# Inverse's step products moved out of a three-buffer scratch ring, and the FFN's gate product on POOL in rounds 16 to 20

## The chip, the cores and the metric

The kernel runs on one core of a Trainium2 chip. The metric is device time in microseconds of one execution. The time before is 573.6 us, the median of three runs (573.47 to 574.25).

## The reference, cut to what matters

One decoder block on x of 256 tokens and 1,024 features, in float32. Everything that the change touches is in these lines:

```python
h = x @ W_in                                   # split into q,k,v,z,... of two attentions
v = silu(causal_dwconv(h_v))                   # 8 heads of 128 features
# gated DeltaNet, chunks of 64 tokens, 8 heads x 4 chunks = 32 systems
a_mat = I + strictly_lower(k_beta k^T * decay)  # 64 x 64 each
sol   = triangular_solve(a_mat, rhs)
...
# ConvGLU, 2 x 2816 columns
u = causal_dwconv(x @ ffn_w_up) + b;  u_gate, u_val = split(u)
f = (silu(u_gate) * u_val) @ ffn_w_down
x = layer_norm(alpha * x + f)
```

## The kernel before

**Products.** Every weight chunk is 128x1024 float32, streamed from HBM by the SP queue into a ring of six `raw` buffers. ACT writes its rounded part `hi` (line 192), DVE the rest `lo` (line 197); `hi` and `lo` have three buffers each. A feature product `mm_feat` (lines 319 to 321) is 24 matmuls of 256 columns into one of two PSUM buffers `pg`; the buffer is free again when ACT and DVE have read it.

**Convolution.** After each q, k or v product, `conv` has ACT write the scaled product into a scratch tile `cv` (line 146) and DVE add three shifted terms to it (line 351, three instructions, each reading `pg` in PSUM and `cv` in SBUF). A `Silu` on ACT follows one product later. In the FFN the same helper makes `ug` and `uv` with two shifted terms each.

**Scratch ring.** `scr()` hands out tiles of 128x512 from one ring of three buffers (`tag="scr", bufs=3`), whatever their name: `cv`, `ug`, `uv`, `hp`, `A`, `y`, `itmp` and others. A request takes the buffer of the third request before it, and waits for that one's last use.

**Order of the work.** All engines run in program order; the Python code writes that order out. The feature products are the backbone. The attention pieces are generators that `pump()` advances by a step after each product, and the table `WAITS` says how many pumps a step is held back. So what PE, ACT and DVE do for the attention stands in their queues at a fixed place among the products.

**The inverse.** `delta()` inverts the triangular systems. The diagonal 16x16 blocks are inverted first, on POOL, by 15 elimination steps (lines 580 to 585): step j multiplies a column of the block with a row of the inverse so far into `itmp` (line 581) and subtracts that from the rows below in `VN` (line 583), at most 8x8 = 64 columns. The result goes out to HBM and back in two other layouts (lines 589 and 592, two DMAs each from the POOL queue); ACT and DVE spread these into `T` and `TT`, both parts of the tile `LT` (ACT at line 146, DVE at line 602), and PE starts the next level of blocks from them at line 615. While POOL works, PE computes the products v0, v1, ... `itmp` is requested from the ring just before the requests of `hp`, of v0's `cv` and of v1's `cv`.

**The attention's memory.** `AT` is a tile of 128x4608 float32: the input at first, then weight chunks, later the attention's exponentials, `e6` (columns 4096 to 4455) and `er` (4456 to 4515). Columns 4096 to 4607 also hold squares of q and k for the norms (line 452), which PE reads before the inverse begins (line 458).

**The FFN.** Round j = 0 to 21 makes the products ug and uv of 128 features each. ACT takes `Silu` of ug; DVE multiplies it with uv into f (line 1319); ACT rounds f into `fh` (line 1323); DVE writes the rest `fl` (line 1324). Rounds 1 to 15 also carry the down product of the round before; the seven last down products (15 to 21) run after round 21, from chunks that are split in rounds 20, 21 and behind them into `YD`, `latemisc`, `latev` and the ring. In rounds 2 to 9 POOL does two 128x256 operations a round (`affine1`, lines 1260 and 1261); in rounds 10 to 21 it has no work.

Of the kernel before, what the change touches and what calls it, by code (L numbers as in the profile page):

```python
# [10 lines left out]
OP = mybir.AluOpType  # L11
# [7 lines left out]
NFF = FF // 128  # L19
# [30 lines left out]
TAIL = 7  # L50
# [49 lines left out]
class Body:  # L100
# [363 lines left out]
    def delta(self):  # L464
        nc = self.nc
# [105 lines left out]
        nc.gpsimd.dma_start(sl.rearrange("u p j -> p u j"), Lc)  # L571
        yield from self.wait("lw")
        nc.gpsimd.dma_start(vf[:, 256:512], sl.rearrange("u (b i) j -> (u b) (i j)", b=8))
        tmp = self.scr("itmp")
        nc.vector.memset(Xi[:, 0], 0.0)
        nc.vector.memset(vf[:, 512:768:17], 1.0)
        yield from self.wait("inv")
# [448 lines left out]
    def run(self):  # L1026
        nc, A = self.nc, self.A
# [203 lines left out]
        def first_up(w, t):  # L1231
            wt = up0[w].rearrange("p (k m) -> p k m", k=8)
            ts = slice(128 * t, 128 * t + 128)
            for k in range(8):
                nc.tensor.matmul(pg0[w][:, ts], wt[:, k], x1T[:, k, ts], start=(k == 0), stop=(k == 7))
# [22 lines left out]
        def affine1(n):  # L1258
            t, sl = n // 4, slice(256 * (n % 4), 256 * (n % 4) + 256)
            nc.gpsimd.tensor_tensor(x1[:, t, sl], res[:, t, sl], lnp[:, 0, sl], op=OP.mult)  # L1260
            nc.gpsimd.tensor_tensor(x1[:, t, sl], x1[:, t, sl], lnp[:, 1, sl], op=OP.add)
# [25 lines left out]
        def down(j, ns=range(5)):  # L1287
            if j == 0:
                for n in range(4):
                    pd[n] = self.ps("pdn")  # L1290
                pd[4] = self.psum.tile([128, 512], F32, name="pdn", tag="o", bufs=1)
            if j not in dch:
                dch[j] = self.next_chunk("dn", j)
            for n in ns:
                down_mm(j, n)
            if ns[-1] == 4:
                self.done_chunk("dn", j)
                self.ahead(most=1 if j > NFF - TAIL + 1 else 3)

        for j in range(NFF):  # L1300
            uu = []
            for w, n in enumerate(("ug", "uv")):
                if j:
                    hi, lo = self.next_chunk(n, j)
                    pg = self.mm_feat(hi, lo, X)
                    self.done_chunk(n, j)
                else:
                    first_up(w, 1)
                    self.done_chunk(n, 0)
                    pg = pg0[w]  # L1310
                c = w * NFF + j
                u = self.scr(n)[:, :256]
                self.conv(pg, u, fcw[:, c], fcb[:, c:c + 1])
                uu.append(u)
                if j + w < NFF:
                    self.ahead(most=1 if j > NFF - TAIL + 1 else 3)
            self.act(uu[0], uu[0], AF.Silu)
            f = uu[0]
            nc.vector.tensor_tensor(f, uu[0], uu[1], op=OP.mult)
            if j == NFF - 1:  # L1320
                self.ahead(most=1)
            fh, fl = Y[:, 0, j % 8], Y[:, 1, j % 8]
            nc.scalar.copy(fh, f)
            nc.vector.tensor_tensor(fl, f, fh.bitcast(F32), op=OP.subtract)
            fs[j] = (fh, fl)
            self.ahead(most=1 if NFF - 1 > j > NFF - TAIL + 1 else 3)
            if 0 < j <= NFF - TAIL:
                down(j - 1)
            if 1 < j < 10:
                affine1(j - 2)  # L1330
# [192 lines left out]
```

## Time and profile before

| | us |
|---|---|
| median of three runs | 573.6 |
| the profiled execution | 573.08 |
| its span, first to last instruction | 571.3 |
| PE busy | 554.5 |
| DVE busy | 394.1 |
| ACT busy | 306.7 |
| POOL busy | 110.3 |

The profiled execution took 1.8 us more than its span, the part before the first and after the last instruction. Busy time is the sum of an engine's instructions, overlaps counted once. Times in the rows are counted from the start of the span. In a timeline, a row's start and length are followed by the engine, the line of the code, the tiles (written <- read), the count and, in brackets, the idle time of the engine before it with what ended it.

### The profile page before, as it was taken

How to read it: one execution, taken by the hardware profiler on the slowest of the kernel's cores; microseconds unless marked ns; L12 is line 12 of the kernel's file. 1: busy time of each engine (PE TensorE's matmuls, PEld its weight loads, DVE VectorE, ACT ScalarE, POOL GpSimd, SP SyncE). 2: the span in 40 equal slices, each digit the busy share in tenths (PEclk: the TensorE clock that was granted, in tenths of full speed). 3: DMA queues.
4: the chain of work that ended last, by engine and by line, in shares of the span. 5: the costliest groups of instructions: out<-in, count | busy, mean ns of one | idle time of the engine just before them, and what ended most of it. 6: DMA issues, size and time to landing. Idle time of an engine off the chain costs nothing.

```text
span 571.3 us, 11612 instructions
## 1 busy us (share of the span) xinstructions
PE 554.5 (97%) x4585; PEld 508.8 (89%) x4585; DVE 394.1 (69%) x683; ACT 306.7 (54%) x575; POOL 110.3 (19%) x160
## 2 busy tenths in 40 slices
PE   8999999999799999999999999999999999999994
PEld 6999999988798898888898898899999999999974
DVE  2888745766686563467657487788777777778884
ACT  4656544624464446564677344465655555556651
POOL 2466632017401130004001000068000000000003
PEclk9999999999899999999999999999999999999998
DMA  8985548765552233223354645735655555555601
GB/s 317 406 305 180 190 146 278 287 211 185 145 182 93 76 112 111 76 73 112 112 185 128 242 148 183 258 102 180 209 185 191 191 180 192 186 189 172 200 3 73
DMA packets 28182, 99.94 MB, mean 175 GB/s; under 512 B 3340, under 2 KB 3996, under 8 KB 27740
## 3 DMA queue, kind: packets, MB, share of 16 engines
q1 hardware_dynamic: 27312, 95.94, 49.1%
q0 software_dynamic: 672, 2.93, 1.7%
q8 instruction: 36, 0.59, 0.4%
q10 hardware_dynamic: 144, 0.33, 0.1%
q14 instruction: 18, 0.15, 0.1%
HBM read 97.33 MB, written 1.46 MB: 173 GB/s over the span
## 4 chain that ended last, share of the span: by engine, by line
PE 77%; DVE 9%; ACT 6%; POOL 3%; issue 2%; DMA 2%; POOLq 0%; SPq 0%; DVEq 0%; ACTq 0%
PE pg L319 18%; PE pg L321 17%; PE pg L320 17%; PE pdn L1284 3%; PE pdn L1285 3%; PE pdn L1283 3%; DVE lo L197 2%; ACT hi L192 2%; PE poa L959 2%; PE pwo L1002 1%; PE pwo L1001 1%; PE pwo L1000 1%; ACT AT L146 1%; POOL itmp L581 1%; POOL VN L583 1%
## 5 line engine op out<-in xcount | busy, mean ns | idle before, releaser
L197 DVE TENSOR_TENSOR lo<-raw,hi 128x1024 fp32r<-128x1024 f32 (+1 forms) x147 | 179.2, 1221 | 75.3 <-ACT hi L192 74.4
L192 ACT CAST hi<-raw 128x1024 fp32r<-128x1024 f32 (+1 forms) x151 | 154.6, 1028 | 36.5 <-PE pg L320 9.8
L319 PE MATMUL pg<-X,hi 128*128 128x256 f32 x496 | 144.3, 291 | 4.8 <-ACT cv L146 4.8
L321 PE MATMUL pg<-X,lo 128*128 128x256 f32 x496 | 140.3, 283 | 0.0
L320 PE MATMUL pg<-X,hi 128*128 128x256 f32 x496 | 140.2, 283 | 0.0
L319 PE MATMUL pg<-Y,hi 128*128 128x256 f32 x400 | 113.0, 283 | 0.0
L320 PE MATMUL pg<-Y,hi 128*128 128x256 f32 x400 | 112.7, 282 | 0.0
L321 PE MATMUL pg<-Y,lo 128*128 128x256 f32 x400 | 112.5, 281 | 0.0
L319 PEld LDWEIGHTS pg<-X,hi 128*128 128x128 f32 x496 | 94.1, 190 | 9.7 <-ACT cv L146 4.9
L320 PEld LDWEIGHTS pg<-X,hi 128*128 128x128 f32 x496 | 94.2, 190 | 0.3 <-issue 0.2
L321 PEld LDWEIGHTS pg<-X,lo 128*128 128x128 f32 x496 | 94.1, 190 | 0.1
L320 PEld LDWEIGHTS pg<-Y,hi 128*128 128x128 f32 x400 | 75.3, 188 | 0.3 <-issue 0.2
L319 PEld LDWEIGHTS pg<-Y,hi 128*128 128x128 f32 x400 | 75.3, 188 | 0.2 <-issue 0.2
L321 PEld LDWEIGHTS pg<-Y,lo 128*128 128x128 f32 x400 | 75.3, 188 | 0.0
L351 DVE SCALAR_TENSOR_TENSOR cv<-pg,ppk,cv 128x255 f32<-128x255 f32 (+2 forms) x72 | 34.6, 481 | 17.4 <-ACT cv L146 15.7
L1359 POOL TENSOR_TENSOR NQ<-NQ,AT 128x512 f32<-128x512 f32 x2 | 2.6, 1298 | 159.7 <-ACT NQ L146 159.7
L1284 PE MATMUL pdn<-lo,X 128*128 128x512 f32 (+1 forms) x90 | 31.6, 351 | 0.0
L1283 PE MATMUL pdn<-hi,X 128*128 128x512 f32 (+1 forms) x90 | 31.5, 350 | 0.0
L1285 PE MATMUL pdn<-hi,X 128*128 128x512 f32 (+1 forms) x90 | 31.4, 349 | 0.0
L910 POOL TENSOR_SCALAR AT<-AT,sums 128x128 f32<-128x128 f32 (+1 forms) x12 | 10.9, 918 | 95.3 <-DVE ec L903 48.4
L351 DVE SCALAR_TENSOR_TENSOR uv<-pg,ppk,uv 128x255 f32<-128x255 f32 (+1 forms) x44 | 21.2, 481 | 11.3 <-ACT uv L146 10.1
L146 ACT ACTIVATE cv<-pg,ppk 128x256 f32<-128x256 f32 x24 | 11.4, 474 | 32.2 <-PE pg L321 26.4
(353 smaller groups left out, 925.8 us busy)
## 6 DMA issues: line engine op xcount, KB each, us to landing
raw<-in_w SPq DMA_DIRECT2D x156, 512.0 KB, 3.4
AT<-in_w SPq DMA_DIRECT2D x12, 512.0 KB, 6.4
Z<-in_w SPq DMA_DIRECT2D x4, 512.0 KB, 7.8
AT<-in_first SPq DMA_DIRECT2D x3, 512.0 KB, 6.6
V<-in_xk POOLq DMA_DIRECT2D x1, 1024.0 KB, 5.5
KD<-in_lnp POOLq DMA_DIRECT2D x1, 1024.0 KB, 6.8
AT<-in_lnp SPq DMA_DIRECT2D x1, 1024.0 KB, 8.1
AT<-in_first SPq DMA_DIRECT2D x2, 256.0 KB, 3.4
```

Of the source, the lines that this page charges most:

```text
L146: self.nc.scalar.activation(out, in_, func, **kw)
L192: nc.scalar.copy(hi[:, o:o + n], raw[:, o:o + n])
L197: nc.vector.tensor_tensor(lo[:, :n], raw[:, :n], hi[:, :n].bitcast(F32), op=OP.subtract)
L319: nc.tensor.matmul(pg, hi[:, k], src[:, 0, k], start=(k == 0), stop=False)
L320: nc.tensor.matmul(pg, hi[:, k], src[:, 1, k], start=False, stop=False)
L321: nc.tensor.matmul(pg, lo[:, k], src[:, 0, k], start=False, stop=(k == 7))
L351: nc.vector.scalar_tensor_tensor(dst[:, s:], pg[:, :S - s], cw[:, n - 1 - s:n - s], dst[:, s:], op0=OP.mult, op1=OP.add)
L910: (nc.vector, nc.gpsimd)[b].tensor_scalar(e, e, w, None, op0=OP.mult)
L959: nc.tensor.matmul(po, self.VT[:, b % 2, c0:c0 + 128], PT[:, b].rearrange("p i q -> p (i q)"), start=False, stop=(b == bs[-1]))
L1283: nc.tensor.matmul(p, fh[:, ts], hi[:, sl], start=(j == 0), stop=False)
L1284: nc.tensor.matmul(p, fh[:, ts], lo[:, sl], start=False, stop=False)
L1285: nc.tensor.matmul(p, fl[:, ts], hi[:, sl], start=False, stop=(j == NFF - 1))
```

## The change

The step products of the inverse go to columns 4516 to 4579 of `AT`, in place of a tile of the scratch ring; nothing else in the inverse is touched. In the FFN the product f of rounds 16 to 20 is given to POOL (gpsimd), in place of DVE. `TAIL` is 7 and `NFF` is 22. Counts, sizes and the order of the program are otherwise the same.

```diff
-        tmp = self.scr("itmp")
+        tmp = self.AT[:, 4516:4580]
...
             self.act(uu[0], uu[0], AF.Silu)
             f = uu[0]
-            nc.vector.tensor_tensor(f, uu[0], uu[1], op=OP.mult)
+            eng = nc.gpsimd if NFF - TAIL < j < NFF - 1 else nc.vector
+            eng.tensor_tensor(f, uu[0], uu[1], op=OP.mult)
```

## Rows read from the trace of the kernel before

**Rows 1.** The page's part 1: busy time, share, instructions of each engine.

```profile
PE 554.5 (97%) x4585; PEld 508.8 (89%) x4585; DVE 394.1 (69%) x683; ACT 306.7 (54%) x575; POOL 110.3 (19%) x160
```

**Rows 2.** Waits of PE, whole span: us in total, times, longest.

```profile
PE pg L319 <- ACT cv L146: 4.8, 1, 4.8
...
PE pdn L1284 <- DVE latev L197: 0.5, 1, 0.5
```

**Rows 3.** Timeline of PE, 138 to 152: start, us, line, tiles, [idle before, releaser].

```profile
141.92 0.28 PE L320 MATMUL pg<-X,hi 128*128 128x256 f32 x1
142.04 0.28 PE L321 MATMUL pg<-X,lo 128*128 128x256 f32 x1
147.07 0.55 PE L319 MATMUL pg<-X,hi 128*128 128x256 f32 x1 [4.76 <-ACT cv L146]
...
150.39 0.29 PE L319 MATMUL pg<-X,hi 128*128 128x256 f32 x1
```

**Rows 4.** Timeline of ACT, 130 to 165 us.

```profile
133.20 0.37 ACT L785 COPY hp<-ph 128x256 f32<-128x256 f32 x1 [0.39 <-PE ph L780]
...
137.76 1.28 ACT L141 ACT_TABLE_LOAD   x1
144.90 0.47 ACT L146 ACTIVATE cv<-pg,ppk 128x256 f32<-128x256 f32 x1 [5.86 <-POOL VN L583]
...
161.58 1.71 ACT L146 ACTIVATE LT<-VN,cpk 128x256 f32<-128x256 f32 x4
```

**Rows 5.** Timeline of DVE, 130 to 152 us.

```profile
138.15 1.27 DVE L197 TENSOR_TENSOR lo<-raw,hi 128x1024 fp32r<-128x1024 f32 x1
...
140.31 0.22 DVE L803 TENSOR_TENSOR hid<-phs,hex 128x60 f32<-128x60 f32 x1
145.41 1.52 DVE L351 SCALAR_TENSOR_TENSOR cv<-pg,ppk,cv 128x255 f32<-128x255 f32 x3 [4.88 <-ACT cv L146]
```

**Rows 6.** Windows, 147.07 to 150.20: PE, PEld, DVE, ACT, POOL busy, PEclk, DMA.

```profile
147.07:150.20 3.13, 3.13 (x15) 3.13 (x15) 3.06 (x5) 1.17 (x2) 2.05 (x2) 0.50 0.55 170
```

**Rows 7.** Timeline of POOL, 130 to 152 us.

```profile
138.42 1.17 POOL L581 TENSOR_TENSOR itmp<-VN 128x64 f32<-128x64 f32 x1
139.67 0.32 POOL L583 TENSOR_TENSOR VN<-VN,itmp 128x64 f32<-128x64 f32 x1
...
144.65 0.22 POOL L583 TENSOR_TENSOR VN<-VN,itmp 128x15 f32<-128x15 f32 x1
...
148.15 2.33 POOL L592 DMA_DIRECT2D VN<-tscr  x2 [1.19 <-DMA tscr<-VN]
```

**Rows 8.** Line 592, the loads of both inverse layouts: time to landing.

```profile
DMA to landing us min/median/max: 4.9/5.3/5.7
```

**Rows 9.** Timeline of PE, 157 to 172 us.

```profile
165.79 1.15 PE L615 MATMUL pa<-LT 64*64 64x64 f32 x32
```

**Rows 10.** Timeline of DVE, FFN round 18.

```profile
525.20 1.23 DVE L197 TENSOR_TENSOR lo<-raw,hi 128x1024 fp32r<-128x1024 f32 x1
526.51 1.00 DVE L351 SCALAR_TENSOR_TENSOR uv<-pg,ppk,uv 128x255 f32<-128x255 f32 x2
527.45 1.23 DVE L197 TENSOR_TENSOR lo<-raw,hi 128x1024 fp32r<-128x1024 f32 x1
528.59 0.42 DVE L1319 TENSOR_TENSOR ug<-ug,uv 128x256 f32<-128x256 f32 x1
```

**Rows 11.** Timeline of ACT, the cast of f in round 18.

```profile
529.04 0.41 ACT L1323 CAST X<-ug 128x256 fp32r<-128x256 f32 x1 [1.31 <-DVE ug L1319]
```

**Rows 12.** Timeline of POOL, FFN rounds 2 to 9.

```profile
390.07 0.73 POOL L1261 TENSOR_TENSOR LT<-LT,KD 128x256 f32<-128x256 f32 x1
...
396.80 1.60 POOL L1261 TENSOR_TENSOR LT<-LT,KD 128x256 f32<-128x256 f32 x1
```

**Rows 13.** Timeline of DVE, the same rounds.

```profile
396.25 1.55 DVE L197 TENSOR_TENSOR lo<-raw,hi 128x1024 fp32r<-128x1024 f32 x1
```

**Rows 14.** The chain that ended last, FFN round 20: start, us, what.

```profile
539.98 0.43 DVE ug L1319
```

## The prediction, made before the changed kernel was run

> **What bounds the kernel now.** I read the page's totals first: PE is busy for 97% of the span [rows 1], so the time is PE's work plus the few holes in it, and an edit counts only where it closes or opens a hole. The list of PE's waits then shows which holes there are. One is far larger than the rest, 4.8 us in one piece, before a feature product; one of 0.5 us sits in the last down products, behind DVE's split of the chunk `latev` [rows 2]. The timelines of the engines around the large hole tell what is late there, the windows what it did to PE's clock.
>
> PE begins a matmul every 0.12 us up to 142.04, and the next one, the first of v3, at 147.07 [rows 3]. Its PSUM buffer is v1's, so v1's convolution has to be over. ACT's part of that convolution is the row at 144.90: ACT stood idle for 5.86 us until POOL's line 583 was done [rows 4]. The convolution reads nothing that POOL writes. What ties them is the ring: `itmp`, `hp` (the row at 133.20), v0's `cv`, v1's `cv`; the fourth request gets `itmp`'s buffer, and POOL's last step ends at 144.65 + 0.22 = 144.87 [rows 4, 7]. So PE waits for DVE's three terms, they for ACT, ACT for a buffer. After the hole the granted clock is 0.50 for 3.13 us, the lower level of 1.2 GHz [rows 6], and the sixteenth matmul comes at 150.39 [rows 3].
>
> **First edit: the ring.** Without `itmp` in it, v1's `cv` takes a buffer whose last reader was done long before. I replay the queues. ACT: the table load ends at 137.76 + 1.28 = 139.04 [rows 4]; v1's product ends about 24 x 0.12 = 2.9 us before v2's, near 139.3; ACT's part is done before 140. DVE: line 803, the instruction before the convolution in its queue, ends at 140.53 [rows 5]. The three terms take 1.52 us [rows 5], so they end at 142.07. PE started 147.07 - 146.93 = 0.14 us after their end, which gives 142.21 for v3, where it would start at 142.16 with no wait at all. Saved: 147.07 - 142.21 = 4.86 us.
>
> With a hole of 0.05 us I take the clock to stay up. Fifteen matmul starts then take 15 x 0.12 = 1.80 us in place of 150.39 - 147.07 = 3.32 [rows 3]. Saved: 1.52 us. Together 6.38 us.
>
> What is late next? From v3 on, each product gives DVE three terms and one `lo`, 1.52 + about 1.2 us [rows 5], against 2.9 us of PE: it fits, narrowly. The inverse does not move with PE. It even slows down, because two `lo` of DVE now fall into it. The step at 138.42 shows the price: it ran into a `lo` of DVE and took 1.17 us, the next one of the same size took 0.32 [rows 5, 7]. Two such meetings cost 2 x 0.85 = 1.70 us. The second load back (line 592) started half of 2.33 us after 148.15, at 149.31, and the slower of the two landed 5.7 us after its start [rows 7, 8]; now 149.31 + 1.70 + 5.7 = 156.7. ACT reads the two loads in four instructions from 161.58 [rows 4], now from 155.20, the second load half-way through, at 156.06: it waits for 0.65 us and ends near 157.6. PE's first use of the spread blocks, line 615 at 165.79 [rows 9], moves to 159.41. So 1.8 us of cover are left and I price this at nothing; if the load landed 3 us later, 1.2 us of the gain would be gone.
>
> The new home costs nothing by itself: the same two POOL instructions per step, the same columns. The norms' squares in these columns were read long ago, and `e6` and `er` end at column 4515.
>
> **Second edit: f on POOL.** In rounds 17 to 20 PE never waits, and the other engines follow it with little to spare. In round 18 (each round is 5.69 us, 48 matmuls): a first `lo` ends at 526.43, the two terms of uv start at 526.51, the second `lo` at 527.45 ends at 528.68, f starts at 528.59, overlapped with its end [rows 10], and ACT's `fh` starts at 529.04 [rows 11]. `fh` opens the next round: behind it in ACT's queue stand the next ug and the next `hi`, behind that `hi` DVE's first `lo`. DVE starts an instruction up to 0.08 us before the reported end of the one before (528.59 against 528.68), so the loop has 526.51 - 526.35 = 0.16 us to spare in a round.
>
> POOL's multiply needs uv's terms, and by then DVE is in the second `lo`. In rounds 2 to 9 POOL ran operations of this very shape beside the same `lo`: the one at 396.80 ended at 398.40, 0.60 us after the `lo` of 396.25 had ended at 397.80 [rows 12, 13]. Undisturbed it takes 0.73 [rows 12]. I take 0.60 after the `lo`, since it is the same shape, engine and neighbour: 528.68 + 0.60 + 0.03 (ACT's row at 144.90 began 0.03 after POOL's end at 144.87 [rows 4, 7]) = 529.31 for `fh`, 0.27 us later than before. DVE's own saving of 0.42 us goes into waiting: its next instruction, `fl`, waits for `fh`. Five rounds with 0.16 spare in the four passages between them: 5 x 0.27 - 4 x 0.16 = 0.71 us of delay on `fh` of round 20. PE keeps pace there, but f of round 20 stands on the chain that ended last [rows 14]: behind it come the split of a `YD` chunk, `latemisc`, then `latev`, for which PE already waits 0.5 us [rows 2]. From there each delay reaches the end. Cost: 0.71 us.
>
> Bounds. Below: if the `lo` did not hold POOL up, f would be ready before DVE's `lo` ends, and the most to be won is PE's 0.5 us wait. Above: the slowest such POOL row, 1.60 us, counted from the end of the `lo`, makes the delay 1.27 a round and 5 x 1.27 - 0.64 = 5.7 us in all.
>
> A rule speaks against this edit. The Trainium skill, "SBUF — State Buffer", section "Who interferes with whom", says that a DVE instruction with two SBUF inputs and a GpSimd one that reads SBUF exclude each other for the whole instruction. By that the multiply would begin only at the end of the `lo` and take all of its 0.73 us, the delay would be 0.40 a round and the cost 5 x 0.40 - 0.64 = 1.36 us, in place of 0.71. The rows agree on the exclusion and differ by 0.13 us, and the sum goes by the rows.
>
> **The sum.** -6.38 + 0.71 = -5.67 us. The profiled execution took 573.08 us (571.3 of span and 1.8 around it), which gives 567.4; it lies 0.5 us under the median of the runs, and from 573.6 the same sum gives 567.9, which I forecast.
>
> **The rivals.**
> - The multiply takes its full length after the `lo`: 1.36 us lost, 573.6 - 6.38 + 1.36 = 568.6. For it: nothing says that the 0.60 holds where DVE idles afterwards. Against: the rows of rounds 2 to 9. Chance 0.15.
> - The inverse comes too late. The loads back now run beside a steadier weight stream. Landing in 1.5 to 2 times 5.7 us puts PE's line 615 at 160.4 to 163.3, 1.0 to 3.9 us late: 568.9 to 571.8. For it: at line 615 the cover falls from 165.79 - 155.0 - 0.9 = 9.9 us to 1.8. Against: the change adds no bytes to move. Chance 0.12.
> - POOL is not held up by the `lo`, and the tail's 0.5 us closes: 566.7. Against it: every row of POOL beside a `lo`. Chance 0.07.
> - The ring edit does not free ACT, because the wait at 144.90 has another cause or `AT`'s other users now hold POOL: 573.6 + 0.71 = 574.3. Against it: the only link from POOL to that instruction is the buffer. Chance 0.03.
> - Slower, by the five multiplies alone: they are in the loop of ACT and DVE, and the first edit is paid back when 5 x delay - 0.64 = 6.38, a delay of 1.40 us a round, which is a multiply that ends 1.73 us after the `lo`. At 2.0 us it gives 574.9. For it: POOL rows of up to 1.6 us. Against: these contain the waiting for the `lo`, which the sum counts already. Chance 0.03.
>
> **The numbers.** The forecast has the remaining 0.60. The range runs from the concurrent case, 566.6, to the middle of the late inverse, 570.2; outside are most of what is slower and the worst late data, under 0.15. About 0.2%, 1.15 us, can be told from no change: faster 0.93 (all of the first four cases but the very late inverse), same 0.03, slower 0.04.
>
> **What the profile after should show.** No wait of ACT for POOL at v1's convolution; v3's first matmul near 142.2 and a granted clock of 1.00 behind it; line 615 near 159.4 with no idle time before it; two steps of the inverse near 1.2 us where there were 0.3. In rounds 16 to 20, POOL rows at line 1320 of 1.2 to 1.6 us, each ending about 0.6 us after a `lo`, `fh` slipping from round to round by about 0.1 us, and PE waiting near 1.2 us for `latev` in place of 0.5. The forecast is wrong if the hole reappears before v4 to v7 or at line 615, if DVE cannot follow the products of v, or if PE waits inside rounds 17 to 21.

## The result, and the profile after

The changed kernel took 570.15 us (median of five runs, 568.28 to 570.92), the kernel before beside it 574.16 us (five runs, 573.47 to 574.53). The ratio is 0.9929, with a 95% interval of 0.991 to 0.9949: 4.0 us faster by the medians, where 5.67 were forecast. The profiled execution took 568.28 us, 566.5 of it span, at a mean granted clock of 0.995; it is the fastest of the five. The busy time of PE is what it was in [rows 1], DVE has given 2.1 us away and POOL has 10.3 more:

```profile
PE 554.3 (98%) x4585; PEld 507.9 (90%) x4585; DVE 392.0 (69%) x678; ACT 306.9 (54%) x575; POOL 120.6 (21%) x165
```

To see where the time went I cut each profile at four starts on PE: the first matmul of v0 (line 319), the first use of the inverse's spread blocks (line 615), the second group of transposes behind the attention (line 1202), and the first matmul that had waited for `latev` (line 1284). Times in us; what the experiments changed is told below.

| kernel | start of v0 | v0 to 615 | 615 to 1202 | 1202 to latev | latev to end | span |
|---|---|---|---|---|---|---|
| before | 133.06 | 32.73 | 209.62 | 172.31 | 23.58 | 571.3 |
| after | 132.95 | 26.28 | 210.93 | 172.87 | 23.47 | 566.5 |
| after, a second time | 133.42 | 26.50 | 211.96 | 172.85 | 23.57 | 568.3 |
| ring edit alone | 134.12 | 26.50 | 211.46 | 172.35 | 23.57 | 568.0 |
| POOL edit alone | 132.85 | 34.19 | 209.84 | 172.90 | 23.42 | 573.2 |
| ring edit, loads from SP | 133.98 | 26.30 | 209.66 | 172.33 | 23.33 | 565.6 |
| ring edit, inverse 4 steps shorter | 134.33 | 26.30 | 209.58 | 172.34 | 23.55 | 566.1 |
| f of round 20 alone | 132.78 | 33.19 | 209.63 | 172.56 | 23.44 | 571.6 |
| f of rounds 16 to 19 alone | 132.97 | 33.06 | 209.58 | 172.54 | 23.45 | 571.6 |
| f of rounds 10 to 14 instead | 134.11 | 32.74 | 209.46 | 172.32 | 23.57 | 572.2 |

The change gained 6.45 us between v0 and line 615, and gave back 1.31 between 615 and 1202 and 0.56 between 1202 and `latev`. How far such a difference can be trusted shows in the stretch from 1202 to `latev`: in the five kernels that have f on DVE in rounds 16 to 20 it lies between 172.31 and 172.35. The start of v0 varies from run to run by over a microsecond in these executions, with edits that come only later; it is no part of the change.

**Where the hole was.** ACT's timeline, 139 to 143 us, with the line that answers to the one at 144.90 in [rows 4]; then PE's, with v3's first matmul, the one that came at 147.07 in [rows 3]; then the windows behind it (columns as in [rows 6]).

```profile
139.40 0.48 ACT L146 ACTIVATE cv<-pg,ppk 128x256 f32<-128x256 f32 x1 [0.46 <-PE pg L321]
...
142.25 0.47 ACT L146 ACTIVATE cv<-pg,ppk 128x256 f32<-128x256 f32 x1 [1.12 <-PE pg L321]
```

```profile
142.05 0.29 PE L319 MATMUL pg<-X,hi 128*128 128x256 f32 x1
...
159.23 1.15 PE L615 MATMUL pa<-LT 64*64 64x64 f32 x32
```

```profile
142.00:147.00 5.00, 5.00 (x44) 5.00 (x44) 4.77 (x8) 3.45 (x6) 4.31 (x10) 1.00 0.61 221
147.00:150.00 3.00, 3.00 (x27) 3.00 (x26) 2.78 (x6) 1.73 (x3) 1.40 (x3) 1.00 0.71 242
```

ACT's only waits there are for PE's own products; PE has no idle time before v3 and the granted clock stays at 1.00, the upper level of 2.4 GHz.

**What came late instead.** POOL's timeline, with the last step of the inverse, its write (line 589) and the two loads back (line 592), to be held against [rows 7]; then ACT's first use of what is loaded, and what stands behind it in the queues of ACT and DVE.

```profile
141.85 1.27 POOL L583 TENSOR_TENSOR VN<-VN,AT 128x55 f32<-128x55 f32 x1
...
144.58 1.09 POOL L581 TENSOR_TENSOR AT<-VN 128x28 f32<-128x28 f32 x1
...
146.36 0.22 POOL L583 TENSOR_TENSOR VN<-VN,AT 128x15 f32<-128x15 f32 x1
...
147.58 1.12 POOL L589 DMA_DIRECT2D tscr<-VN  x2 [0.30 <-POOL VN L586]
151.16 1.17 POOL L592 DMA_DIRECT2D VN<-tscr  x1 [2.46 <-DMA tscr<-VN]
152.57 1.16 POOL L592 DMA_DIRECT2D VN<-tscr  x1 [0.24 <-issue]
```

```profile
156.88 1.71 ACT L146 ACTIVATE LT<-VN,cpk 128x256 f32<-128x256 f32 x4 [1.76 <-DMA VN<-tscr]
158.49 0.40 ACT L146 ACTIVATE Z<-cv 128x256 f32<-128x256 f32 x1
158.80 0.46 ACT L146 ACTIVATE cv<-pg,ppk 128x256 f32<-128x256 f32 x1
```

```profile
159.29 1.51 DVE L351 SCALAR_TENSOR_TENSOR cv<-pg,ppk,cv 128x255 f32<-128x255 f32 x3 [1.10 <-ACT cv L146]
```

ACT, which had not waited here [rows 4], stands idle for 1.76 us; behind its four instructions in its queue stand a `Silu`, the convolution of the next product and, at 159.16, a `hi`. So DVE waits 1.10 us for ACT. The chain that ended last, followed back from line 889, runs through exactly this place (start, us, what; its middle part is work of DVE and ACT alone):

```profile
147.58 3.30 DMA tscr<-VN
150.88 0.28 issue
151.16 5.61 DMA VN<-tscr
156.88 0.72 ACT LT L146 x2
...
158.90 0.37 ACT cv L146
159.29 0.49 DVE cv L351
...
162.56 1.23 DVE lo L197
...
179.99 0.61 DVE A L617
180.65 0.70 PE psa L889 x2
```

The trace of before has the same chain already, only that it starts from PE and not from the loads: from 160.27 to 185.95 it is work of ACT and DVE, one instruction behind the other, and at its end PE waits 0.61 us (the chain that ended last, before):

```profile
160.05 0.13 PE pg L321
160.27 0.48 ACT cv L146
...
185.29 0.61 DVE A L617
185.95 0.70 PE psa L889 x2
```

So ACT and DVE had next to no slack in this stretch even before the change. PE feels the late loads only 12 us behind line 615. Its timeline shows two waits that it did not have before, ahead of lines 552 and 615 (the second use), and 0.84 us ahead of line 889, where it had waited 0.61:

```profile
169.27 1.15 PE L621 MATMUL pu<-A,LT 64*64 64x64 f32 x32
171.73 1.35 PE L552 MATMUL pv<-cpk,Z 128*128 128x128 f32 x8 [0.38 <-ACT AT L146]
176.18 1.15 PE L615 MATMUL pa<-LT 64*64 64x64 f32 x32 [0.22 <-DVE LT L628]
...
180.65 0.70 PE L889 MATMUL psa<-KC,NQ 128*128 128x256 f32 x2 [0.84 <-DVE A L617]
```

The same four in the timeline of before:

```profile
175.83 1.15 PE L621 MATMUL pu<-A,LT 64*64 64x64 f32 x32
177.84 1.09 PE L552 MATMUL pv<-cpk,Z 128*128 128x128 f32 x8
181.71 1.15 PE L615 MATMUL pa<-LT 64*64 64x64 f32 x32
...
185.95 0.70 PE L889 MATMUL psa<-KC,NQ 128*128 128x256 f32 x2 [0.61 <-DVE A L617]
```

Counted from the first line 615 (165.79 before, 159.23 after) they come at 10.04, 12.05, 15.92 and 20.16 us before, and at 10.04, 12.50, 16.95 and 21.42 after: late by 0, 0.45, 1.03 and 1.26 us, nearly all of the 1.31.

**f on POOL.** Round 18 again: DVE's second `lo`, POOL's multiply and ACT's `fh`, which answer to [rows 10] and [rows 11]; then PE's wait for `latev`.

```profile
522.30 1.22 DVE L197 TENSOR_TENSOR lo<-raw,hi 128x1024 fp32r<-128x1024 f32 x1
```

```profile
522.68 1.43 POOL L1320 TENSOR_TENSOR ug<-ug,uv 128x256 f32<-128x256 f32 x1 [4.31 <-ACT ug L146]
```

```profile
524.14 0.41 ACT L1324 CAST X<-ug 128x256 fp32r<-128x256 f32 x1 [1.59 <-POOL ug L1320]
...
535.74 0.41 ACT L1324 CAST X<-ug 128x256 fp32r<-128x256 f32 x1 [1.61 <-POOL ug L1320]
```

```profile
543.03 0.50 PE L1284 MATMUL pdn<-latev,X 128*128 128x512 f32 x1 [0.66 <-DVE latev L197]
```

The multiply ends at 522.68 + 1.43 = 524.11, that is 0.59 us after the end of the `lo` at 523.52, and `fh` starts 0.03 later.

### The profile page after: what moved, and what is told of

It reads as the page before. It is cut to its first block, busy times and chain, and to the rows that moved or that the text cites. A ratio compares the mean times of both kernels' runs of the same rounds, so it can differ in the third digit from the quotient of the medians.

```text
span 566.5 us, 11605 instructions
## 1 busy us (share of the span) xinstructions
PE 554.3 (98%) x4585; PEld 507.9 (90%) x4585; DVE 392.0 (69%) x678; ACT 306.9 (54%) x575; POOL 120.6 (21%) x165
## 4 chain that ended last, share of the span: by engine, by line
PE 77%; DVE 8%; ACT 5%; DMA 4%; POOL 3%; issue 2%; SPq 0%; DVEq 0%; ACTq 0%; POOLq 0%
PE pg L319 17%; PE pg L321 17%; PE pg L320 17%; PE pdn L1284 3%; PE pdn L1285 3%; PE pdn L1283 3%; DVE lo L197 2%; ACT hi L192 2%; PE poa L959 2%; DMA raw<-in_w 1%; POOL AT L581 1%; PE pwo L1001 1%; PE pwo L1002 1%; PE pwo L1000 1%; POOL VN L583 1%
## 5 line engine op out<-in xcount | busy, mean ns | idle before, releaser
L1320 POOL TENSOR_TENSOR ug<-ug,uv 128x256 f32<-128x256 f32 x5 | 7.2, 1448 | 135.3 <-ACT ug L146 135.3
L1324 ACT CAST X<-ug 128x256 fp32r<-128x256 f32 x22 | 8.9, 407 | 34.6 <-DVE ug L1320 26.7
```

## The experiments

The theory after the result (L, where the expectations use letters): the ring edit gave the full 6.4 us, and the part missing is the loads back of the inverse, which now hold ACT (and DVE behind it) up, and delay PE some 12 to 21 us later. The rivals were that the POOL multiplies cost 2.3 us in place of 0.71 (M), and that the loss behind line 615 does not come from the loads at all (S). The kernel before was run again beside each group of kernels; its median was 573.97, 574.0 and 574.22 us.

**One edit at a time.** The first kernel has the ring edit, with f on DVE as before; the second has f on POOL, with `itmp` in the ring.

```diff
 e1 (against after)
-            eng.tensor_tensor(f, uu[0], uu[1], op=OP.mult)
+            nc.vector.tensor_tensor(f, uu[0], uu[1], op=OP.mult)
 e2 (against after)
-        tmp = self.AT[:, 4516:4580]
+        tmp = self.scr("itmp")
```

> The ring edit alone, f stays on DVE. Theory L (the loads back of the inverse land too late for ACT and DVE, which takes 1.3 us of the gain in the profiled run of the changed kernel and some 2 us more in its other runs; the POOL multiplies cost 0.6 us): 4.7 us faster than before, 569.5, and ACT still waits 1 us or more for VN<-tscr. Rival M (the POOL multiplies cost 2.3 us, and the ring edit gives its full 6.4): 6.4 us faster, 567.8.

> POOL's multiplies alone, the ring as before. Theory L: 0.6 us slower than before, 574.7, PE's wait for latev near 0.7 to 1.1 us. Rival M: 2.3 us slower, 576.4.

Measured: the ring edit alone 569.71 us against 573.97, ratio 0.993 (0.9916 to 0.9944), 4.3 us gained; the POOL edit alone 574.94, ratio 1.0018 (1.0008 to 1.0029), 1.0 us lost. The table gives the places: the ring edit alone loses 1.84 us between 615 and 1202 and nothing behind; the POOL edit alone loses 0.59 us between 1202 and `latev`. That is the rival of 2.3 us gone. The rest of the second kernel's loss in its profile is the old hole, which cost it more than it did before: the windows behind it show the lower clock until about 153, some 6 us, where it was little more than the 3.13 us of [rows 6] before.

```profile
146.88:150.00 3.12, 3.12 (x15) 3.12 (x15) 3.05 (x5) 1.17 (x2) 2.04 (x2) 0.50 0.54 159
150.00:152.00 2.00, 2.00 (x11) 2.00 (x11) 0.55 (x1) 0.00 (x0) 1.02 (x3) 0.50 1.02 229
152.00:155.00 3.00, 3.00 (x23) 3.00 (x23) 1.99 (x4) 1.73 (x3) 0.00 (x0) 0.82 0.60 191
```

**The reads two products later.** `back0` is the number of pumps that the reads of the loads are held back. With more of it the data would be there, at the price of a later start of everything behind; once on the changed kernel (e3) and once on the ring edit alone (e4).

```diff
-WAITS = dict(back0=6, ...
+WAITS = dict(back0=8, ...
```

> The changed kernel with the reads of the loads back (ACT and DVE) placed two products later in their queues, 8 pumps in place of 6. Theory L: neither ACT nor DVE waits for VN<-tscr, 1.3 to 3 us faster than the changed kernel, near 568, and its runs lie closer together. Rival M: no difference from the changed kernel, 570.1.

> The ring edit with f on DVE and the reads of the loads two products later. Theory L: the whole 6.4 us, 567.3 to 567.8, 0.6 us faster than the same with f on POOL. Rival M: the same as the ring edit alone, 567.8, and 2.3 us faster than the same with f on POOL.

Measured: 577.78 us against 573.97, ratio 1.0063 (1.0045 to 1.0082), and 576.71, ratio 1.0049 (1.0032 to 1.0065). No theory had foreseen that both would be slower than the kernel before. In the first one's profile ACT still waits for the loads, 0.83 and 0.32 us; the write took 4.6 to 4.8 us to land there and the loads 6.7 to 6.9. The second one's ACT no longer waits for the loads, but PE now waits further on for the attention's work, which has moved back by two products (PE's waits in that kernel):

```profile
PE psa L889 <- DVE ec L880: 3.5, 2, 1.8
...
PE pg L319 <- ACT YD L727: 1.7, 1, 1.7
PE psa L889 <- ACT AT L945: 1.6, 1, 1.6
```

These runs say that a later place is worse; they don't tell the theories apart.

**The same loads, from another queue.** On the ring edit alone, line 592 is issued by SP instead of POOL.

```diff
-            nc.gpsimd.dma_start(vf[:, 256 * w:256 * w + 256]...
+            nc.sync.dma_start(vf[:, 256 * w:256 * w + 256]...
```

> The ring edit alone, with the two loads back (line 592) issued by SP in place of POOL. Theory L: without POOL's 1.2 us of issue for each of them they land 1 to 2 us earlier, ACT's wait shrinks from 1.9 us to below 0.9, and the time falls by 0.5 to 1.3 us against the ring edit alone, 568.4 to 569.2. If the landing itself takes longer from SP's queue (it is shared with the weights), nothing is won: 569.7 or more. Rival S: no difference, 569.7.

Measured: 567.65 us against 574.0, ratio 0.9887 (0.987 to 0.99), the best of all versions that do the whole work, and 2.1 us below the ring edit alone. The loads take 1.38 us of SP's queue, where they took 2.45 of POOL's in the ring edit alone, and land in 3.0 to 3.5 us in place of 5.6 to 5.8. ACT reads them with no idle time before it, and at `psa` PE is back at the 0.61 us of before (SP's queue from 140 to 165 us; line 592's time to landing; ACT; PE):

```profile
140.38 0.33 SPq L170 DMA_DIRECT2D raw<-in_w  x1
151.74 1.38 SPq L592 DMA_DIRECT2D VN<-tscr  x2
153.21 10.52 SPq L170 DMA_DIRECT2D raw<-in_w  x8
```

```profile
DMA to landing us min/median/max: 3.0/3.3/3.5
```

```profile
156.06 1.71 ACT L146 ACTIVATE LT<-VN,cpk 128x256 f32<-128x256 f32 x4
```

```profile
180.44 0.70 PE L889 MATMUL psa<-KC,NQ 128*128 128x256 f32 x2 [0.61 <-DVE A L617]
```

From 615 to 1202 it takes 209.66 us, as before the change. This is what the theory of the late loads wants. It doesn't show that the queue by itself makes the loads land sooner, for the edit changed two things. SP issues in order, so while it stood at the loads, waiting for the write ahead of them, it issued no weights: none from 140.38 to 153.21, where the ring edit alone issued one every 3 us or so. The write ahead of the loads then had the DMA engines nearly to itself (a share of 0.30 while it was under way, in place of 0.80) and landed in 2.7 to 3.0 us, in place of 3.3 to 3.8. Which part of the earlier landing is the queue and which the pause of the weights is not separated.

**A shorter inverse.** Two kernels leave out the last four of the 15 elimination steps (the inverse is then incomplete); both stand on the ring edit alone. The first shortens the loop; the second keeps the loop and its pumps, and leaves out only the instructions.

```diff
 e5
-        for j in range(15):
+        for j in range(11):
 e9
+            if j < 11:
                 nc.gpsimd.tensor_tensor(t, ...
                 nc.gpsimd.tensor_tensor(Xi[:, 0, j + 1:16, 0:m], ...
```

> The ring edit alone, and of the inverse's 15 steps the last four left out (8 POOL instructions, some 3 us), so that its blocks are not fully inverted. Theory L (ACT and DVE have no cover for loads that land late): the loads land some 3 us earlier, ACT's wait of 1.9 us for VN<-tscr is gone, and so are PE's added waits (0.6 us before line 552, 0.2 before line 615, 0.2 more before line 889) and 0.4 more: 1.3 us faster than the ring edit alone, 568.4. Rival S (those 1.3 us are the chain of DVE and ACT after it, slow by itself and only uncovered by the ring edit): as the ring edit alone, 569.7.

> The ring edit alone, the last four steps of the inverse left out (its blocks are not fully inverted), but with all five pump waits between steps kept, so that the reads of the loads stay at their place in the queues of ACT and DVE. Theory L: the loads land some 2.5 to 3.5 us earlier, ACT does not wait for them, the stretch from line 615 to the transposes of line 1202 falls back from 211.5 us (ring edit alone) to 209.6, near 568.0 in all. Rival S (the stretch is longer because DVE and ACT are slow by themselves): the stretch stays near 211 us, 569.7.

Measured: the first 573.35 us against 574.0, ratio 0.9989 (0.9978 to 1.0001). It missed, since two pumps fell away with the steps: the reads moved two products forward, and the loads came later against them, not earlier. It does show what a late load costs when it is bad enough, for ACT waited 5.00 us and the old hole was back on PE:

```profile
154.58 1.77 ACT L146 ACTIVATE LT<-VN,cpk 128x256 f32<-128x256 f32 x4 [5.00 <-DMA VN<-tscr]
```

```profile
158.72 0.55 PE L319 MATMUL pg<-X,hi 128*128 128x256 f32 x1 [4.96 <-ACT cv L146]
```

The second, with the reads in their place, took 567.5 us against 574.22, ratio 0.9873 (0.9852 to 0.9894). The loads are issued at 148.57 in place of 152.42 and still take 6.2 to 6.4 us from POOL's queue, yet ACT does not wait, and 615 to 1202 takes 209.58 us. Two edits with little in common but the earlier landing remove the loss, and in this one neither the queue nor the weight stream was touched; the rival without the loads falls.

**The changed kernel again**, beside these, to see whether its loss behind line 615 is always the 1.31 us of the first profile.

> The changed kernel once more, beside the others. Theory L and the sum of the traces (the POOL multiplies cost 0.56 us): 570.3, that is 0.4 to 0.7 us slower than the ring edit alone in its own runs; its profile shows ACT waiting 1 to 3 us for VN<-tscr, and differs from the first one mainly in the first 120 us, where loads from HBM set the start.

Measured: 570.03 us against 574.0, ratio 0.9926 (0.9913 to 0.9939). In this execution ACT waits twice for the loads, 1.08 and 1.52 us, and the loss between 615 and 1202 is 2.34 us. The profiled execution of the result was a lucky one in that.

**Which multiplies cost.** With the ring as before, f goes to POOL in round 20 alone (e8), in 16 to 19 (e11, one run), and in rounds 10 to 14 in place of 16 to 20 (e10).

```diff
 e8
+            eng = nc.gpsimd if j == NFF - 2 else nc.vector
 e11
+            eng = nc.gpsimd if NFF - TAIL < j < NFF - 2 else nc.vector
 e10
+            eng = nc.gpsimd if 10 <= j < 15 else nc.vector
```

> The ring as before, f on POOL in round 20 alone. By the step that the delay of 0.27 us of one multiply reaches the end through round 20: in the trace the stretch from the transposes (line 1202) to PE's wait for latev grows by 0.2 to 0.3 us against before, where all five rounds gave 0.59; the time is not to be told from before, 573.9 to 574.3. Rival (each round adds the same, and round 20 has no special place): 0.11 us.

> The ring as before, f on POOL in rounds 16 to 19, round 20 on DVE. By the slip of the loop from round to round the fh of round 20 is 0.3 us late, and so is latev: the stretch from line 1202 to PE's wait for latev is 172.6, where all five rounds gave 172.9 and round 20 alone 172.56. Rival (only round 20 matters): 172.3.

> The ring as before, f on POOL in rounds 10 to 14, which carry a down product each and where ACT waits more than 1 us for PE in each round. If the cost of the edit is the tight loop of rounds 17 to 20 and the chain through round 20: each fh is late by 0.27 us and nothing adds up, the stretch from line 1202 to PE's wait for latev stays at 172.3 us, the time as before. Rival (each multiply on POOL costs its 0.1 us anywhere): 172.8 to 172.9.

Measured: 573.96 us against 574.0 (ratio 1.0, 0.999 to 1.001); 573.38 in one run; 574.14 against 574.22 (1.0011, 0.9993 to 1.0029; two of its ten runs, 576.85 and 577.74, raise the ratio above that of the medians). Between 1202 and `latev` round 20 alone adds 0.25 us, rounds 16 to 19 add 0.23, all five 0.59, and rounds 10 to 14 add 0.01 (one profile each). The two parts show in different places. With round 20 alone PE's wait for `latev` grows from 0.46 to 0.72 us; with rounds 16 to 19 it stays at 0.47, and the loss is in the rounds themselves. In rounds 10 to 14 POOL's multiplies take as long as later (the first of them):

```profile
466.36 1.46 POOL L1320 TENSOR_TENSOR ug<-ug,uv 128x256 f32<-128x256 f32 x1 [67.07 <-ACT ug L146]
```

So the multiply on POOL is not dear by itself. What costs is the place: the rounds from 16 on and the chain behind them to `latev`, where nothing takes the delay up.

## Why the prediction was right or wrong

- **The hole and its cause: right.** Without `itmp` in the ring ACT waits only for PE. ACT's part of v1's convolution came at 139.40 (forecast near 139.3), v3 at 142.05 (142.21). The gain up to line 615 was 6.45 us in the first profile and 6.23 in the second, for 6.38. The clock stayed up, as the sum had it. (The end of DVE's three terms is 140.53 + 1.52 = 142.05, not 142.07; nothing hangs on the 0.02.) The 1.52 us for the clock are those of one profile: in the other four profiles with this hole the lower clock lasted 3.3 to 6.1 us, so its price varies by more than a microsecond.
- **The slower inverse: right.** Two steps met a `lo` and took 1.27 and 1.09 us. The last step ended at 146.36 + 0.22 = 146.58, which is 1.71 us later than before, for 1.70; POOL had run 0.10 us ahead of before until then, so the meetings cost 1.8.
- **The late loads, priced at nothing: wrong, and this is the step that failed.** Two things were off in it, and the loss in its size comes from both. One is the landing. The loads were forecast to issue at 149.85 and 151.01 (the rows of before plus 1.70). They issued at 151.16 and 152.57, because the write ahead of them took 3.3 us to land and not the 2.0 of before. ACT waited 1.76 us, not 0.65, and ended at 158.59, not 157.6. The other is where the cover was read. The step took it at PE's line 615, found 1.8 us, and line 615 did come with no wait (159.23, forecast 159.41). But ACT and DVE have cover of their own, and from here to `psa` it is next to nothing: the chain that ended last is unbroken work of these two from the loads to 180.65. The chain of before shows it already, from 160.27 to 185.95, so even the 0.65 us of waiting that the step forecast had next to no slack to go into (read from that chain; no run has a wait of that size). What ACT lost at 156.88 was handed on and became 1.26 us of PE 21 us later. The rival "the inverse comes too late" named the cause and, at 568.9 to 571.8, holds the result, but it had the loss at line 615 and only with a landing 1.5 times as long. The loads landed in 5.0 to 5.6 us, no longer than before; what was longer was the write ahead of them.
- **f on POOL: right, the size a little high.** The multiply of round 18 ended 0.59 us after its `lo` (0.60 in the sum), those of rounds 16, 17 and 19 0.58 to 0.60. From round 16 to 20 `fh` went from 512.65 to 535.74, in steps of 5.77 us where a round had 5.69: a slip of 0.08 us a round, for 0.11. (528.59 against 528.68 is 0.09, not 0.08: with 0.17 us to spare the sum would have been 0.67.) The cost is 0.56 us (0.59 alone) for 0.71. By the rule of the Trainium skill ("SBUF — State Buffer", "Who interferes with whom") the prediction had estimated 1.36; the trace agrees that DVE's two-input instruction and POOL exclude each other (a step of 0.3 us took 1.27 beside a `lo`), but after a `lo` the multiply took 0.59 and not its undisturbed 0.73 [rows 12]. What was wrong is that PE keeps pace in these rounds: the wait for `latev` grew by only 0.20 us, to 0.66 (forecast near 1.2), and the other 0.36 was lost ahead of it, nearly all in rounds 17 to 21, in gaps too small for the list of waits. The kernels with f on POOL in round 20 alone and in rounds 16 to 19 alone show the two parts one at a time.
- **The sum.** In place of -6.38 + 0 + 0.71 = -5.67, the second profile of the changed kernel gives -6.23 + 2.34 + 0.54 = -3.35, the first -6.45 + 1.31 + 0.56 = -4.58; the medians say -4.0. That 570.15 us still lies inside the range, by 0.05, is luck as far as this sum goes: the upper end, 570.2, was drawn through the middle of the late inverse, a rival given a chance of 0.12 (the middle of 568.9 and 571.8 is 570.35, and the lower end, 566.6, is the 566.7 of its rival).

Not settled: why the write of the inverse took 3.3 to 4.0 us to land in the changed kernel, against 2.0 before. In the five profiles with the old hole it landed in 2.0 us each time, at a DMA share of 0.33 to 0.36 while it was under way, and in the first profile of the changed kernel the share was 0.75, which fits a busier stream. But the share does not order the times: with the loads on SP it was 0.30 and the write took 2.7 to 3.0 us, and with the inverse four steps shorter it was 0.92 and the write took 2.7 to 2.8. Nothing was run that changes the weight stream alone.

## What to carry to other kernels

When an edit lets one engine run ahead, price each datum that does not move with it at the queue of the engine that waits for it, in order, and follow what stands behind it there; the first use on the bounding engine may show cover that the chain through the others does not have. Where the chain that ended last runs through those others already, as here in the trace of before, they have none to give. A helper that hands out buffers from one ring ties work together that shares no data, so look at the order of requests before believing a wait's name. Once a wait for a small load is the bound, try another queue for its issue: here that was worth 2.1 us, half of what the whole change gave. Then look at what else that queue carries, since what stands behind the load in it waits too: here 12 us without a new weight load, which the six `raw` buffers covered (PE had no idle time in them).

## What the runs showed of the hardware

- The same two loads from HBM took 4.1 to 6.9 us from issue to landing in the twelve profiles in which POOL issued them (5.0 to 5.6 in the first of the changed kernel), with some 1.17 us of issue each, and 3.0 to 3.5 us in the one in which SP did, with 0.39 and 0.89 us of issue. In that one the weights paused as well, so the difference is not the queue's alone.
- A hole of the same 4.7 to 4.8 us did not cost the same clock each time. Behind it PE started a matmul every 0.21 us, at a granted clock of 0.50, for 3.3 us in the kernel before, 3.3 with f of rounds 10 to 14, 4.1 with rounds 16 to 19, 4.4 with round 20 alone and 6.1 with the POOL edit alone, with PE busy all the while. The stretch from v0 to line 615 grows in the same order: 32.73, 32.74, 33.06, 33.19, 34.19.
